# A matmul-tanh-multiply kernel: float32r operands, DMA transposes and 512-column matmuls in place of bf16, TensorE transposes and 384 columns

## The chip, the cores and the metric

The kernel runs on one core of a Trainium2 chip. The metric is device time in microseconds; lower is better. A profiled execution gives a span, from the first to the last instruction, some 2 us below the timed value. Runs of one kernel mostly agree within 0.3%; a run more than 1.5% above the fastest of its kernel is marked slow and left out of comparisons.

Words used below. TensorE multiplies matrices and writes its results into banks of a memory called PSUM. VectorE, ScalarE and GpSimd do the other arithmetic; SyncE, ScalarE and GpSimd also issue DMAs, the transfers between memories, each on a queue of its own. The changed kernel and the experiments pin their instructions to program order, so on an engine or a queue what was written first runs first. float32r is the 4-byte type that the changed kernel gives its matmuls; widening is the copy from bf16 to it. A DMA transpose turns x while it copies it (the crossbar). The DMA share adds up the times of all DMA packets and divides by 16 engines' time; these times can overlap.

## The reference

```python
x: (16, 512, 1024) float32;  w1, w2: (1024, 768) float32
y1 = np.matmul(x, w1); y2 = np.matmul(x, w2)
return (np.tanh(y1) * y2).astype(np.float32)
```

The 16 x 512 rows of x make 64 tiles of 128 rows. Each needs x transposed in eight blocks of 128 x 128, then eight accumulation steps for 768 columns of each weight.

## The kernel before

Weights are loaded as float32 and cast by an engine. x is cast to bf16 by its load, transposed on TensorE, and copied out of PSUM block by block.

```python
nc.sync.dma_start(w1_f, w1r)
nc.sync.dma_start(w2_f, w2r)
# ...
nc.any.tensor_copy(w1_b, w1_f)
nc.any.tensor_copy(w2_b, w2_f)
# ...
for mt in range(MT):
    nc.gpsimd.dma_start(x_b, xf[mt])              # float32 -> bf16
    for ko in range(KO):
        nc.tensor.transpose(pt, x_b[:, ko * P:(ko + 1) * P], ident)
        nc.any.tensor_copy(xT[:, ko, :], pt)
    for nt in range(NT):                          # 2 x 384 columns
        for ko in range(KO):
            nc.tensor.matmul(ps1, xT[:, ko, :], w1_b[:, ko, ns:ns + N_TILE], ...)
            nc.tensor.matmul(ps2, xT[:, ko, :], w2_b[:, ko, ns:ns + N_TILE], ...)
        nc.scalar.activation(t1, ps1, Tanh)
        nc.vector.tensor_tensor(o, t1, ps2, mult)
        nc.sync.dma_start(of[mt, :, ns:ns + N_TILE], o)
```

## Time and profile before

| | before |
|---|---|
| time, us (median of 2) | 414.78 |
| span, us | 413.0 |
| TensorE busy | 92% |
| start to start of 384-column matmuls, ns | 162.5 |
| period of one x tile, us | 6.00 |
| mean clock granted to TensorE, share of full | 0.996 |

The period is the useful line: 64 tiles pass one after the other, and whatever repeats in each tile counts 64 times. The profile lines themselves stand in the prediction.

### The profile page before, as it was taken

The page shows a single profiled execution, that of the slowest core. Times are in us where ns is not written, and L with a number is a line of the kernel's source. Part 1 is how long each engine was busy: PE and PEld are TensorE (multiplying, and loading weights), DVE is VectorE, ACT ScalarE, POOL GpSimd, SP SyncE. Part 2 cuts the span into 40 slices and gives each one's busy share as a digit, 9 for nine tenths or more (in the row PEclk, how much of TensorE's full clock was granted, in tenths as well). Part 3 has the DMA queues.
Part 4 walks back from the last instruction along what each step waited for, and adds up shares of the span by engine and source line. Part 5 has one row for each costly group of instructions (what it writes and reads, how often), then busy time and mean ns, then how long its engine had stood idle before and what let it go on. Part 6 is the DMA issues. An engine that isn't in the chain of part 4 may idle for free.

```text
span 413.0 us, 6572 instructions
## 1 busy us (share of the span) xinstructions
PE 381.2 (92%) x2560; PEld 235.9 (57%) x2560; DVE 107.2 (26%) x316; ACT 128.7 (31%) x455; POOL 36.8 (9%) x70
## 2 busy tenths in 40 slices
PE   1496999999999999999999999999999999999995
PEld 0253666666666666666666666666666666666663
DVE  0301232232223232222323232232223232222322
ACT  1434132332333233323323332332333233323322
POOL 2400001110110011011101101110110011011000
PEclk9998999999999999999999999999999999999999
DMA  8971345444444543444354345434444543444221
GB/s 255 294 264 40 101 123 119 107 108 116 110 109 101 129 109 104 110 108 117 95 128 108 106 106 120 111 102 116 109 110 102 128 106 106 108 110 116 71 77 58
DMA packets 29760, 48.67 MB, mean 118 GB/s; under 512 B 3104, under 2 KB 19488, under 8 KB 29728
## 3 DMA queue, kind: packets, MB, share of 16 engines
q0 software_dynamic: 9216, 16.78, 24.7%
q1 hardware_dynamic: 20512, 31.47, 21.1%
q8 instruction: 20, 0.33, 0.3%
q14 instruction: 12, 0.10, 0.1%
HBM read 39.85 MB, written 25.17 MB: 157 GB/s over the span
## 4 chain that ended last, share of the span: by engine, by line
PE 86%; DMA 7%; DVE 3%; ACT 1%; issue 1%; SPq 0%
PE ps L79 41%; PE ps L77 38%; PE pt L67 7%; DMA w_f<-in_w_dram 7%; DVE xT L68 3%; ACT w_b L53 1%; DVE o L84 0%; ACT t L82 0%; SPq L48 0%
## 5 line engine op out<-in xcount | busy, mean ns | idle before, releaser
L79 PE MATMUL ps<-w_b,xT 128*128 128x384 bf16 x1024 | 326.7, 328 | 4.2 <-ACT w_b L53 4.2
L77 PE MATMUL ps<-w_b,xT 128*128 128x384 bf16 x1024 | 327.0, 328 | 1.6 <-DVE w_b L52 1.6
L82 ACT ACTIVATE t<-ps 128x384 f32<-128x384 f32 x128 | 62.7, 490 | 266.8 <-PE ps L77 263.3
L77 PEld LDWEIGHTS <-xT 128*128 128x128 bf16 x1024 | 100.6, 98 | 77.4 <-issue 19.7
L79 PEld LDWEIGHTS <-xT 128*128 128x128 bf16 x1024 | 100.5, 98 | 67.9 <-issue 6.0
L84 DVE TENSOR_TENSOR o<-t,ps 128x384 f32<-128x384 f32 x128 | 70.9, 554 | 179.7 <-ACT t L82 158.5
L67 PE MATMUL pt<-ident,x_b 128*128 128x128 bf16 x512 | 64.0, 223 | 21.5 <-DMA x_b<-in_x_dram 12.5
L68 ACT COPY xT<-pt 128x128 bf16<-128x128 bf16 x325 | 65.6, 271 | 11.7 <-PE pt L67 11.1
L63 POOL DMA_DIRECT2D x_b<-in_x_dram x64 | 36.2, 566 | 342.9 <-PE pt L67 342.5
L68 DVE COPY xT<-pt 128x128 bf16<-128x128 bf16 x187 | 36.0, 221 | 117.5 <-PE pt L67 114.7
L67 PEld LDWEIGHTS <-x_b 128*128 128x128 bf16 x512 | 39.7, 99 | 26.9 <-DMA x_b<-in_x_dram 13.9
L53 ACT CAST w_b<-w_f 128x6144 bf16<-128x6144 f32 x1 | 5.3, 5312 | 1.0 <-DMA w_f<-in_w_dram 1.0
L52 DVE CAST w_b<-w_f 128x6144 bf16<-128x6144 f32 x1 | 3.4, 3361 | 5.1 <-DMA w_f<-in_w_dram 5.1
L68 ACT ACT_TABLE_LOAD x1 | 1.3, 1283 | 0.7 <-PEq L100 0.7
masks.py:199 POOL TENSOR_SCALAR_AFFINE_SELECT ident<-ident 128x128 bf16<-128x128 bf16 x1 | 0.3, 304 | 0.1
masks.py:197 POOL MEMSET ident<- 128x128 bf16 x1 | 0.2, 204 | 0.3 <-POOLq L100 0.3
L100 POOL MEMSET const-float32-0.0<- 128x1 f32 x1 | 0.1, 98 | 0.2 <-issue 0.2
L100 POOL MEMSET const-bfloat16-1.0<- 128x1 bf16 x1 | 0.1, 102 | 0.0
L100 POOL MEMSET const-uint8-127<- 128x1 uint8 x1 | 0.1, 102 | 0.0
L100 POOL MEMSET const-float32-1.0<- 128x1 f32 x1 | 0.1, 98 | 0.0
## 6 DMA issues: line engine op xcount, KB each, us to landing
out_dram<-o SPq DMA_DIRECT2D x128, 192.0 KB, 1.9
x_b<-in_x_dram POOLq DMA_DIRECT2D x64, 256.0 KB, 3.7
w_f<-in_w_dram SPq DMA_DIRECT2D x2, 3072.0 KB, 22.0
```

The source lines that it names most:

```text
L52: nc.any.tensor_copy(w1_b, w1_f)
L53: nc.any.tensor_copy(w2_b, w2_f)
L63: nc.gpsimd.dma_start(x_b, xf[mt])
L67: nc.tensor.transpose(pt, x_b[:, ko * P:(ko + 1) * P], ident)
L68: nc.any.tensor_copy(xT[:, ko, :], pt)
L77: nc.tensor.matmul(ps1, xT[:, ko, :], w1_b[:, ko, ns:ns + N_TILE], start=st, stop=sp)
L79: nc.tensor.matmul(ps2, xT[:, ko, :], w2_b[:, ko, ns:ns + N_TILE], start=st, stop=sp)
L82: nc.scalar.activation(t1, ps1, mybir.ActivationFunctionType.Tanh)
L84: nc.vector.tensor_tensor(o, t1, ps2, mybir.AluOpType.mult)
L100: nc = _bacc.Bacc("TRN2", target_bir_lowering=False, num_devices=1)
```

## The change

The intent is to leave TensorE only real matmuls: no transposes, wider matmuls, no separate weight cast, and a start that works on four tiles while weights arrive. The diff, cut to its core (the removed lines are those shown above):

```diff
+    w_b = [wpool.tile([P, NC, 2, HALF], f32r, name=f"w_b{k}") for k in range(KO)]
+    pin = tc.keep_in_program_order
+    def load_x(mt):                       # tiles x_b and xT are made here; left out
+        pin(nc.gpsimd.dma_start(x_b, xf[mt]))
+        pin(nc.sync.dma_start_transpose(xT, x_b))
+        xR = xrpool.tile([P, KO, P], f32r, tag="xR", name="xR")
+        pin(nc.vector.tensor_copy(xR, xT))
+        xts[mt] = xR
+    def finish(mt, c, ps, o):
+        pin(nc.scalar.activation(t1, ps[:, :HALF], ACT.Tanh))
+        pin(nc.vector.tensor_tensor(o[:, c * HALF:(c + 1) * HALF], t1, ps[:, HALF:], ALU.mult))
+    def store(mt, o):
+        pin(nc.sync.dma_start(of[mt], o))
... start: four tiles and the weights interleaved, matmuls in order of k, then load_x(4), (5), (6) ...
+    for mt in range(HEAD, MT):            # HEAD = 4
+        if mt + AHEAD < MT:               # AHEAD = 3
+            load_x(mt + AHEAD)
+        o = new_o()
+        for c in range(NC):               # 3 chunks: 256 columns of w1 beside 256 of w2
+            ps = bank()
+            for k in range(KO):
+                mm(ps, mt, k, c)
+            finish(mt, c, ps, o)
+        store(mt, o)
```

## The prediction

> **What bounds the kernel now.** I read the busy line and the chain of the page first.
>
> ```profile
> PE 381.2 (92%) x2560; PEld 235.9 (57%) x2560; DVE 107.2 (26%) x316; ACT 128.7 (31%) x455; POOL 36.8 (9%) x70
> ...
> PE 86%; DMA 7%; DVE 3%; ACT 1%; issue 1%; SPq 0%
> PE ps L79 41%; PE ps L77 38%; PE pt L67 7%; DMA w_f<-in_w_dram 7%; DVE xT L68 3%; ACT w_b L53 1%; DVE o L84 0%; ACT t L82 0%; SPq L48 0%
> ```
>
> TensorE is the bound: 79% of the chain is the two matmul lines, 7% the PE transposes, 3% the copies of transposes that PE waits for, and 8% a start spent on the weight load (DMA) and its cast (ACT). No other engine is above 31%. Next, the groups, and the TensorE timeline of one x tile in the steady part.
>
> ```profile
> L79 PE MATMUL ps<-w_b,xT 128*128 128x384 bf16 x1024 | 326.7, 328 | 4.2 <-ACT w_b L53 4.2
> L77 PE MATMUL ps<-w_b,xT 128*128 128x384 bf16 x1024 | 327.0, 328 | 1.6 <-DVE w_b L52 1.6
> L82 ACT ACTIVATE t<-ps 128x384 f32<-128x384 f32 x128 | 62.7, 490 | 266.8 <-PE ps L77 263.3
> L84 DVE TENSOR_TENSOR o<-t,ps 128x384 f32<-128x384 f32 x128 | 70.9, 554 | 179.7 <-ACT t L82 158.5
> L67 PE MATMUL pt<-ident,x_b 128*128 128x128 bf16 x512 | 64.0, 223 | 21.5 <-DMA x_b<-in_x_dram 12.5
> ```
>
> ```profile
> 54.59 0.75 PE L67 MATMUL pt<-ident,x_b 128*128 128x128 bf16 x5
> 55.18 0.32 PE L77 MATMUL ps<-w_b,xT 128*128 128x384 bf16 x1
> 55.35 0.37 PE L67 MATMUL pt<-ident,x_b 128*128 128x128 bf16 x3
> 55.55 0.32 PE L79 MATMUL ps<-w_b,xT 128*128 128x384 bf16 x1
> 55.72 0.32 PE L77 MATMUL ps<-w_b,xT 128*128 128x384 bf16 x1
> ...
> 60.59 0.75 PE L67 MATMUL pt<-ident,x_b 128*128 128x128 bf16 x5
> ```
>
> The 328 ns of a matmul is a latency; what counts is start to start, 0.162 us here. A tile's period is 60.59 - 54.59 = 6.00 us. It holds 32 matmuls, 32 x 0.1625 = 5.20 us, so the eight transposes and their holes cost 0.80 us. The table of windows agrees: 2203 matmuls of both kinds between 64 and 394 us are 55 tiles of 40 in 330 us, at a granted clock of 1.00. Last the start, from the timeline and the DMA part:
>
> ```profile
> 16.90 3.36 DVE L52 CAST w_b<-w_f 128x6144 bf16<-128x6144 f32 x1 [5.11 <-DMA w_f<-in_w_dram]
> 17.62 2.76 POOL L63 DMA_DIRECT2D x_b<-in_x_dram x1 [1.87 <-PE pt L67]
> ...
> 20.31 9.92 PE L77 MATMUL ps<-w_b,xT 128*128 128x384 bf16 x48 [1.64 <-DVE w_b L52]
> ...
> 29.13 5.31 ACT L53 CAST w_b<-w_f 128x6144 bf16<-128x6144 f32 x1 [0.97 <-DMA w_f<-in_w_dram]
> ```
>
> ```profile
> q0 software_dynamic: 9216, 16.78, 24.7%
> q1 hardware_dynamic: 20512, 31.47, 21.1%
> ```
>
> Real matmuls start at 20.31 us, and the second weight is usable only at 34.4. The steady DMA share is about 45%. A detail for later: the issue of an x load, 0.57 us in the mean, took 2.76 us and ended just after a VectorE cast did.
>
> **What the Trainium skill says.** First, "TensorE: Matmul & The Clock Gate", section Back-to-back issue gap: a warm gap is N / 2.4 + 2.5 ns. For N = 384 this is 162.5, and the trace shows 0.162. For N = 512 it is 215.8 ns. Second, the same page under Weight-path perf modes: the fast weight load is on for 128 weights of a type that is not FP32. Its LDWEIGHTS section gives P / 1.2, so 107 ns for 128 columns. The trace has only bf16 loads, 98 ns each, wholly hidden at N = 384; whether a 4-byte load hides it can't say. Third, "FP8 and Floating Point Precision", section TensorE Precision Notes: a reduced-precision form reads 4-byte data and truncates it to FP22, while true FP32 takes four passes. No run here shows the rate of float32r. Fourth, "DMA: Bandwidth & Descriptors", section Latency and other measured facts: a DMA transpose moves 261 GB/s in one kernel, 350 to 400 where contiguous. The trace before has none.
>
> **The change part by part.**
>
> Matmuls. The columns streamed stay the same: 2048 x 384 = 1536 x 512 = 786,432. The compiled program has 1536 weight loads, each just before its matmul, as before in number of two per product, but the float32r load is one run of 128 columns where the bf16 one is four chunks of 32; I read that as the slow load. At 107 ns it fits below a matmul of 216 ns that streams in front of it, so I take it as hidden and float32r as one column a cycle. Then a tile is 24 x 0.2158 = 5.18 us, and all 1536 are 331.5 us. Wider matmuls by themselves save only 512 x 2.5 ns = 1.3 us.
>
> Transposes on PE. All 512 go, with the holes for their copies: 6.00 - 5.18 = 0.82 us a tile, and 60 steady tiles save 49 us. This is the main gain. The 512 copies on ACT and DVE (101.6 us) go too, off the path.
>
> New work on VectorE. One widening of 1024 elements a tile. The weight cast took 3361 ns for 6144 elements, 0.55 ns each, so 0.56 us (estimate), maybe 0.65 with a fixed part. The products are three of 256 columns instead of two of 384, at most 3 x 554 ns. That is 2.3 us of 5.18. ScalarE has at most 3 x 490 = 1.5 us. Eight PSUM banks are filled at 1.73 us each, so eviction has several banks of slack. Beside PE, nothing on the path.
>
> New work on DMA. q0 took 24.7% of 413 us, 102 us over 64 tiles, so an x load costs all engines 1.6 us; q1's 87 us is mostly stores, at most 1.36 us a tile. The transpose writes 0.262 MB, 1.0 us at 261 GB/s. Sum 4.0 of 5.18 us, a share of 77%. It fits with little to spare. x is fetched three tiles, 15 us, ahead, enough for load (3.7 us to landing), transpose (I guess 3 us) and widening in series.
>
> The start. Four x tiles and eight weight slices come interleaved on one queue. An x tile is 1.6 us; a weight slice of two halves is 0.52 MB, about 1.9 us at the 255 to 294 GB/s that the first slices show. The fourth x tile lands after 4 x 1.6 + 3 x 1.9 = 12.1 us plus 2.5 for issue and latency = 14.6; transpose and widening make it 18.3. The last slice lands near 24. The 64 head matmuls go in order of k, so k = 0 ends near 18.3 and seven groups of 8 x 0.216 = 1.73 follow: 30.5, and about 33.5 with a cold clock at first (3 us). The third column block of these tiles, 32 matmuls, 6.9 us, ends at 40.4; its weights (another 2.1 MB) come in by 32 to 34. Tile 4, loaded after them, is ready near 41.2. Before, tile 4 began one period ahead of 54.59, so about 48.6: a gain of 7.4 us.
>
> Sum. 41.2 + 60 x 5.18 = 352.0, plus a tail of 4.6 us, as in the kernel before from its last tanh at 408.4 to 413.0, is a span of 356.6. The timed value was 1.8 us above the span, so 358.4. By differences: 414.8 - 49.2 - 7.4 = 358.2.
>
> **The rivals.**
> (a) float32r streams at half rate, since each element has twice the bytes. Then 1536 x 0.429 = 659 us plus 30 to 40: near 690. For it: nothing in the trace, which has bf16 alone. Against it: the skill's reduced-precision form is one read, and the change chooses 512 columns and pairs the two weights in one moving operand, as one would who knows the rate holds. I give it 8%.
> (b) The slow weight load isn't hidden. Each matmul then costs 216 + 60 to 107 ns: 1536 x 0.276 to 0.323 = 424 to 496, plus 27, so 450 to 525. For it: a transpose of 128 columns, whose stream is a third of the others', costs 0.59 / 5 = 118 ns start to start, so a load isn't free beside a short matmul. Against it: at 384 columns it is free to the nanosecond, and 107 fits in 216. 8%.
> (c) DMA becomes the bound. If the transpose runs at half the 261 GB/s, the sum is 5.0 us a tile, still just under; at a third it is 6.0, and the kernel takes about 41 + 60 x 6.0 + 6 = 407. SyncE issues transposes and stores in one in-order queue, so a slow issue would show there. 9%.
> (d) VectorE's widening holds up the x loads' issue, as the 2.76 us did. At 0.6 us a tile against three tiles of slack it costs nothing.
>
> **Range and chances.** If (a) to (c) all fail, 75%, the time is 349 to 375: below 349 the start would have to take under 18 us of PE time, above 375 would need stalls in the steady part. A mild (c) reaches 395. So 349 to 390. Faster 0.79, within 2% 0.03 (a hard (c)), slower 0.18.
>
> **What would show each step right or wrong.** Right: matmul starts 0.216 us apart in one tile; tile period 5.18 us; about 96% of the steady chain on the one matmul line; no PE idle on xR after tile 4; DMA share 0.7 to 0.8; first dense matmuls near 18 us, tile 4 near 41. Wrong: starts 0.27 to 0.33 apart with weight loads between, rival (b); 0.43 apart, (a); matmuls waiting for xR and, behind it, for the transposes, (c). A late start would be a wait for x or for weight slices in the first 45 us, and moves the result only by its own length.

## The result

The changed kernel took 469.62 us (468.56 to 470.67) against 414.78: slower, ratio 1.133 (95% interval 1.127 to 1.139). Here and below a ratio is the mean time of one kernel's fast runs over that of the other's in the same rounds, so not quite the ratio of the medians quoted. The prediction of 358 us was far off.

The page of the changed kernel: busy time, the chain that ended last by engine and by line, and groups of instructions (busy us, mean ns, idle time before and what ended it).

```profile
PE 374.1 (80%) x1536; PEld 292.6 (63%) x1536; DVE 108.6 (23%) x256; ACT 68.8 (15%) x193; POOL 54.2 (12%) x100
...
DMA 60%; DVE 13%; PE 11%; issue 8%; SPq 5%; POOL 3%; ACT 0%; DVEq 0%; POOLq 0%
DMA xT<-x_b 54%; DVE o L75 12%; PE ps L84 11%; DMA w_b<-in_w_dram 5%; SPq L81 4%; POOL w_b L59 2%; SPq L67 1%; DMA x_b<-in_x_dram 1%; DVE xR L69 1%; POOL x_b L65 0%; ACT t L74 0%; DVEq L69 0%; POOLq L146 0%
...
L84 PE MATMUL ps<-w_b,xR 128*128 128x512 f32 x1536 | 374.1, 402 | 88.6 <-DVE o L75 61.8
...
L69 DVE CAST xR<-xT 128x1024 fp32r<-128x1024 bf16 x64 | 44.4, 694 | 344.4 <-DMA xT<-x_b 344.3
```

The matmuls, 79% of the chain before, are 11% of it now; the DMA transpose is 54%. VectorE sat idle for 344 us until a transpose landed, and TensorE waited for VectorE's product, which frees a PSUM bank. The queue of SyncE has its own waits (us in total, times, longest):

```profile
SPq L81 <- DVE o L75: 295.0, 64, 7.7
```

So the store (L81) waits on its queue for the product, VectorE waits for the transpose, and the transpose (L67) stands on that same queue. The timeline of two turns in the steady part (start us, us taken, engine, line):

```profile
96.84 0.33 SPq L81 DMA_DIRECT2D out_dram<-o  x1
97.26 1.57 SPq L67 DMA_TRANSPOSE xT<-x_b  x1
101.77 0.69 DVE L69 CAST xR<-xT 128x1024 fp32r<-128x1024 bf16 x1 [4.96 <-DMA xT<-x_b]
...
102.38 1.08 DVE L75 TENSOR_TENSOR o<-t,ps 128x256 f32<-128x256 f32 x3
...
103.48 0.33 SPq L81 DMA_DIRECT2D out_dram<-o  x1
...
103.90 1.74 SPq L67 DMA_TRANSPOSE xT<-x_b  x1
```

Read it as a ring. The transpose is issued at 97.26. It lands 4.5 us later. Only then comes the widening, 0.6 us until the products begin, and the three products, whose inputs had long been ready, 1.1 us. Then the store of that tile, and 0.42 us later the next transpose. The turn is 103.90 - 97.26 = 6.64 us. Between 61.55 us (tile 4's first matmul) and the end of matmuls a tile took 6.68 us in the mean, against 6.00 before.

Two smaller things. Inside a tile float32r matmuls start 227 ns apart, not 216. And tile 4 began at 61.55 us, where the kernel before began the matmuls of its tile 4 at 49.40 (the prediction's 48.6 was an estimate).

Where the 54 us of span went: the start, 61.55 - 49.40 = 12.1, and the 60 tiles after it, 401.1 us against 359.1, which is 42; the tail is 0.4 us shorter.

### The profile page after: what moved, and what is told of

Read it like the earlier page. It is cut to its first block, busy times and chain, and to the rows that moved or that the text cites. A ratio compares the mean times of both kernels' runs of the same rounds, so it can differ in the third digit from the quotient of the medians.

```text
span 466.8 us, 4237 instructions
## 1 busy us (share of the span) xinstructions
PE 374.1 (80%) x1536; PEld 292.6 (63%) x1536; DVE 108.6 (23%) x256; ACT 68.8 (15%) x193; POOL 54.2 (12%) x100
## 3 DMA queue, kind: packets, MB, share of 16 engines
q1 hardware_dynamic: 76800, 41.96, 41.2%
## 4 chain that ended last, share of the span: by engine, by line
DMA 60%; DVE 13%; PE 11%; issue 8%; SPq 5%; POOL 3%; ACT 0%; DVEq 0%; POOLq 0%
DMA xT<-x_b 54%; DVE o L75 12%; PE ps L84 11%; DMA w_b<-in_w_dram 5%; SPq L81 4%; POOL w_b L59 2%; SPq L67 1%; DMA x_b<-in_x_dram 1%; DVE xR L69 1%; POOL x_b L65 0%; ACT t L74 0%; DVEq L69 0%; POOLq L146 0%
## 5 line engine op out<-in xcount | busy, mean ns | idle before, releaser
L84 PE MATMUL ps<-w_b,xR 128*128 128x512 f32 x1536 | 374.1, 402 | 88.6 <-DVE o L75 61.8
L84 PEld LDWEIGHTS ps<-w_b,xR 128*128 128x128 f32 x1536 | 292.6, 193 | 169.7 <-DVE o L75 80.1
L74 ACT ACTIVATE t<-ps 128x256 f32<-128x256 f32 x192 | 67.5, 385 | 393.6 <-DVE o L75 316.6
L69 DVE CAST xR<-xT 128x1024 fp32r<-128x1024 bf16 x64 | 44.4, 694 | 344.4 <-DMA xT<-x_b 344.3
L65 POOL DMA_DIRECT2D x_b<-in_x_dram x64 | 34.3, 546 | 346.6 <-DMA xT<-x_b 345.2
L75 DVE TENSOR_TENSOR o<-t,ps 128x256 f32<-128x256 f32 x192 | 69.1, 415 | 10.5 <-ACT t L74 10.5
L59 POOL DMA_DIRECT2D w_b<-in_w_dram x32 | 20.0, 639 | 11.5 <-DMA w_b<-in_w_dram 9.1
```

The source lines that it names most:

```text
L59: pin(nc.gpsimd.dma_start(w_b[k][:, c0:c1, h, :], src[:, k, c0 * HALF:c1 * HALF].rearrange("p (c j) -> p c j", j=HALF)))
L65: pin(nc.gpsimd.dma_start(x_b, xf[mt]))
L69: pin(nc.vector.tensor_copy(xR, xT))
L74: pin(nc.scalar.activation(t1, ps[:, :HALF], ACT.Tanh))
L75: pin(nc.vector.tensor_tensor(o[:, c * HALF:(c + 1) * HALF], t1, ps[:, HALF:], ALU.mult))
L84: pin(nc.tensor.matmul(ps, xts[mt][:, k, :], w_b[k][:, c, :, :].rearrange("p h j -> p (h j)"), start=k == 0, stop=k == KO - 1))
```

## The experiments

The theory: the loss is the order of instructions. On VectorE the widening of tile mt+3 stands ahead of the products of tile mt; on SyncE's queue the transpose of tile mt+4 stands behind the store of tile mt. Together these make a ring with one transpose per turn, whatever the look-ahead. Rivals: DMA transposes or the DMA engines can't do a tile faster; or float32r itself is what costs. All kernels of the experiments were correct, and before was 412.9 to 416.1 us in all their rounds.

| run | what differs from the changed kernel | us, median (n) | ratio to before |
|---|---|---|---|
| changed kernel | | 469.62 (2) | 1.133 |
| e1_widen_late | widening after the products | 386.26 (4) | 0.932 |
| e2_store_act | stores on ScalarE's queue | 466.84 (4, three slow) | |
| e3_bf16_same_copy | bf16, a copy where the widening was | 463.43 (4) | 1.118 |
| e4_bf16_no_copy | bf16, no copy | 368.64 (4) | 0.888 |
| e5_ahead6 | look-ahead 6 instead of 3 | 475.59 (4) | 1.149 |
| e6_f32r_256 | e1 with 256-column matmuls | 405.86 (1) | one look |
| e7_store_act_2xt | e2, two transposed tiles buffered | 400.77 (4) | 0.970 |
| e9_store_act_3xt | e2, three buffered | 393.92 (4, one slow) | 0.948 |
| e9_store_act_5xt | e2, five buffered | 445.50 (4, three slow) | |
| e8_best | e4 with another start | 354.20 (4) | 0.856 |

### e1_widen_late: the same work, another order on VectorE

```diff
 def load_x(mt):                       # tiles 4 and up; the first four as before
     ...
-    pin(nc.vector.tensor_copy(xR, xT))
+    later[mt] = xT
 for mt in range(HEAD, MT):
     ...
     store(mt, o)
+    if mt + AHEAD < MT:
+        widen(mt + AHEAD, later[mt + AHEAD])    # the tensor_copy
```

Tiles 4 to 6 are widened likewise, each after a store of the first four tiles.

> Everything of the changed kernel is kept (float32r, crossbar transposes, their number, place and queue), only the widening of tile mt+3 stands behind the three products of tile mt in VectorE's order instead of ahead of them. Loop theory (the transpose of a tile is issued behind a store that waits for products that wait behind a widening that waits for the transpose before, so one turn of 4.7 + 0.6 + 1.1 + 0.4 us per tile): the loop is cut, a tile takes 24 x 0.227 = 5.44 us, tile 4 starts near 54 instead of 61.5, and the time is about 54 + 60 x 5.44 + 6 = 387 us. Rival, the crossbar or the DMA engines can't do a tile in less than about 6.7 us: the time stays at 460 to 470. Rival, float32r itself makes the loss: no change either.

Measured: 386.26 us, 83 us below the changed kernel, from moving one instruction per tile. The table of windows for 100 to 360 us (busy us and count per engine, granted clock, DMA share, GB/s) has TensorE busy throughout:

```profile
100.00:360.00 260.00, 260.00 (x1149) 215.36 (x1148) 90.35 (x192) 54.92 (x143) 22.62 (x42) 1.00 0.86 165
```

That is 260 / 1149 = 0.226 us a matmul, so 5.44 us a tile. The transposes now take 5.3 us to land, longer than the 4.7 before, and after the start TensorE waits for nothing. Tile 4 starts at 52.0 us. The ring was the main loss; the transposes and the DMA engines can do a tile in 5.44 us (DMA share 0.86 here, 0.68 in the changed kernel between 100 and 400 us).

The new order doesn't abolish the ring, it makes it longer. A turn of the timeline (start us, us taken, engine, line):

```profile
96.62 0.33 SPq L88 DMA_DIRECT2D out_dram<-o  x1
97.04 1.56 SPq L68 DMA_TRANSPOSE xT<-x_b  x1
...
102.06 0.33 SPq L88 DMA_DIRECT2D out_dram<-o  x1
102.35 0.69 DVE L76 CAST xR<-xT 128x1024 fp32r<-128x1024 bf16 x1 [0.32 <-DMA xT<-x_b]
102.48 1.29 SPq L68 DMA_TRANSPOSE xT<-x_b  x1
```

The transpose issued at 97.04 lands when a whole further tile has been multiplied and stored, and VectorE waits 0.32 us for it. By the program's order such a transpose, issued after the products of tile mt, must land before those of tile mt+2; in the changed kernel it was before those of tile mt+1. So a turn may take two tiles, some 10.9 us.

### e3_bf16_same_copy and e4_bf16_no_copy: is it float32r?

```diff
 e3, e4:
-    w_b = [wpool.tile([P, NC, 2, HALF], f32r, ...
+    w_b = [wpool.tile([P, NC, 2, HALF], bf16, ...
 e3:
-    xR = xrpool.tile([P, KO, P], f32r, ...
+    xR = xrpool.tile([P, KO, P], bf16, ...
 e4:
-    pin(nc.vector.tensor_copy(xR, xT)); xts[mt] = xR
+    xts[mt] = xT
```

> Weights cast to bf16 by the loading DMA, and VectorE makes a plain bf16 copy where the widening stood: the loop is whole, float32r is gone. Loop theory: a tile takes the loop's 6.7 us less what the bf16 copy is shorter (0.69 to perhaps 0.4), so about 6.4, and the time is 440 to 455 us though matmuls could be 0.216 us apart. Rival that float32r matmuls are the loss: 5.2 us a tile, about 370 us.

Measured: 463.43 us. With float32r gone and the ring left, almost nothing is gained, so float32r isn't the main loss. The size was off: 440 to 455 was expected. A tile took 6.61 us. The copy is 0.43 us instead of 0.69, but the transposes landed in 4.9 us instead of 4.7, which took most of that back; why they did is open.

> As the run before but without the copy: TensorE reads the transposed bf16 tile, and VectorE waits for no transpose. Loop theory: cut, 24 x 0.216 = 5.18 us a tile, about 50 + 311 + 6 = 367 us. Against the late widening this is float32r's own price, 11 ns x 1536 = 17 us. Rival of a crossbar or DMA limit: above 430.

Measured: 368.64 us, as expected. Against e1 the difference of 17.6 us is mostly float32r's own price in this kernel: 1536 x 11 ns = 17 us. (The widening and the wider weights go too; the 60 tiles after the start account for 15.6 us.) The windows of 100 to 340 us:

```profile
100.00:340.00 240.00, 240.00 (x1114) 108.81 (x1113) 58.56 (x140) 53.52 (x139) 22.24 (x42) 1.00 0.94 174
```

It is 240 / 1114 = 0.215 us a matmul. The DMA share is 0.94. That isn't a distance to a limit: e8_best, with the same steady part, has 0.88 in the same window, and e2_store_act below has 1.26.

### e6_f32r_256: what the 11 ns are

```diff
 e1, after the start:
-            for k in range(KO):
-                mm(ps, mt, k, c)
+            for h in range(2):
+                for k in range(KO):
+                    matmul(ps[:, h * HALF:(h + 1) * HALF], xts[mt][:, k, :], w_b[k][:, c, h, :], ...)
```

> The late widening with 256-column matmuls after the head (twice as many): what the extra 11 ns of a float32r matmul is. A fixed cost per matmul: [...]120 ns start to start. A share of 5 per cent of the streaming: about 115. A weight load that can't be hidden under a short matmul: clearly above 130, up to the 190 ns that its record lasts. The time is then 54 + 60 x 48 x that gap + 6, so 405 us at 120.

Measured: 405.86 us in one look. The windows of 100 to 360 us, and the group of weight loads:

```profile
100.00:360.00 260.00, 260.00 (x2169) 260.00 (x2169) 86.65 (x182) 51.84 (x135) 23.21 (x43) 1.00 0.84 159
...
L139 PEld LDWEIGHTS ps<-w_b,xR 128*128 128x128 f32 x2880 | 345.7, 192 | 0.1
```

It is 260 / 2169 = 0.120 us. No bf16 run has 256 columns; the line through bf16's 162.5 ns at 384 and 215 at 512 puts it at 110 (an estimate). So the extra looks like a fixed 10 to 11 ns per matmul at both widths, not a share of the streaming, and the weight load is otherwise hidden though its record lasts 192 ns (98 with bf16). What the 11 ns are made of no run shows; they can be a part of the weight load.

### e5_ahead6: more look-ahead

```diff
-    AHEAD = 3
+    AHEAD = 6
```

> The changed kernel with x fetched six tiles ahead instead of three, and the buffers for it. Loop theory: look-ahead buys nothing, for each turn of the loop still carries one transpose; only three more tiles lie outside the loop, each 5.44 instead of 6.7 us, so about 465 us, 460 to 468. Rival, a plain latency that more slack would hide: near 385 us.

Measured: 475.59 us, somewhat above the changed kernel. A latency that slack would hide is thus ruled out. The size was a small miss: the widenings of six tiles, not three, now stand on VectorE ahead of the first four tiles' products, so tile 4 began at 77.4 us instead of 61.5; the 60 tiles after it took 8.8 us less than in the changed kernel (392.3 for 401.1), which doesn't make up for that.

### e2_store_act: the other cut, and what came in its place

```diff
-        pin(nc.sync.dma_start(of[mt], o))
+        pin(nc.scalar.dma_start(of[mt], o))
```

> The changed kernel with the output stores issued from ScalarE's queue, so that on SyncE's queue no transpose stands behind a store; VectorE's order as it was. Loop theory: the other link of the same loop is cut, transposes run ahead by their buffers, 5.44 us a tile, 385 to 400 us in all. Rival of a crossbar or DMA limit: 460 to 470, with transposes back to back on the queue. If only the first of the two cuts helped, the loop as stated would be wrong.

Measured: 466.84 us (452.68 to 477.66, only the lowest of four counted as fast). Even that run is far above the 385 to 400 expected: a plain miss. The trace is of a slow run, 473.04 us. From the DMA part of the page, the queue that now holds the transposes alone (packets, MB, share of 16 engines), and the issues (median us to landing):

```profile
q1 hardware_dynamic: 67584, 16.79, 61.6%
...
x_b<-in_x_dram POOLq DMA_DIRECT2D x64, 256.0 KB, 14.6
...
xT<-x_b SPq DMA_TRANSPOSE x64, 19.2
```

With no store ahead of them, several transposes are under way at once and land after 19 us, and the x loads beside them take 14.6 instead of 3.8. The windows of 100 to 400 us have a DMA share above 1, though no more was moved than in the changed kernel (131 GB/s, 130 there):

```profile
100.00:400.00 300.00, 257.50 (x1068) 206.87 (x1067) 73.64 (x171) 43.28 (x129) 22.07 (x41) 0.95 1.26 131
```

VectorE still waits for each of them in order. Either the transposes pile up and hinder each other, or the store's own queue beside them does harm, or the ring was the wrong cause. The next runs tell these apart by letting fewer transposes be under way.

### e7_store_act_2xt, e9_store_act_3xt, e9_store_act_5xt: how many at once

```diff
 e2 with
-    xtpool = ctx.enter_context(tc.tile_pool(name="xtpool", bufs=HEAD + AHEAD))
+    xtpool = ctx.enter_context(tc.tile_pool(name="xtpool", bufs=2))     # or 3, or 5
```

> The run with stores on ScalarE's queue cut the loop and gained nothing, with transposes landing 19 us after issue and DMA busy throughout. Here the same, with two buffers for the transposed bf16 tile instead of seven, so at most two transposes can be under way. If it was transposes piling up in the queue that took the gain, they now land in about 5 us, a tile takes 5.44 and the time is 385 to 400 us. If it was the store's own queue beside the transposes, or if the loop was the wrong cause, the time stays above 440 us.

Measured: 400.77 us. The same two lines with two buffers:

```profile
q1 hardware_dynamic: 67584, 16.79, 28.8%
...
xT<-x_b SPq DMA_TRANSPOSE x64, 5.3
```

The packets of the same bytes took less than half the time in sum (28.8% of 398.5 us is 115 us; 61.6% of 471.3, in the slow run, is 290). A tile takes 5.44 us. So cutting the ring on SyncE's queue does work, if the transposes don't pile up.

> Between the two runs with stores on ScalarE's queue: two buffers of the transposed bf16 tile gave 400.8 us, seven 466.8. Here three. If queued transposes slow each other step by step, the time is a little above 400, up to 420 us, and the 256-byte packets take longer than 28 ns; if there is a threshold above three it is 400 as with two.

Measured: 393.92 us, with one run of 437.88. Three are as good as two; being a little faster is the start, tile 4 at 61.1 us against 67.7.

> The same with five buffers. If the time grows with the number of transposes that may be under way: between that of three buffers and 466.8 us, 430 to 466, with packets between 28 and 69 ns. If only the last buffers hurt: about 400 us.

Measured: 445.50 us (420.45 to 481.68; only the 420.45 counts as fast). By the fast runs, which are one each for five and seven, the times for two, three, five and seven buffers are about 401, 393, 420 and 453. The slow run with three suggests that three isn't always safe; it has no trace. Before stayed between 412.9 and 416.1 us in the same rounds, so the slow runs here may be the pile-up itself rather than a state of the chip; that isn't shown.

Buffers allowed are not transposes under way. Counted in the traces between issue and landing, three were under way for 67% of the time in e2 and 72% with five buffers (both slow runs), for 12% with three buffers, and in e7 one for 75%. That letting them pile up is harmful is shown: with the stores on the same queue, the number of buffers alone makes 401 or 453 us. Whether the transposes hinder each other or meet more x loads (in e2 two or three of these were under way most of the time, in e7 one) isn't told apart, and why their packets take longer is open.

### e8_best: the start

```diff
 e4 with
+    # w_b[k] is [P, 2, N]: each slice loaded as two rows of 768 columns
+    # the first four tiles:
+    pt = pspool.tile([P, KO, P], bf16, tag="ps", name="pt")
+    for k in range(KO):
+        pin(nc.tensor.transpose(pt[:, k, :], xbs[mt][:, k * P:(k + 1) * P], ident))
+    pin(nc.vector.tensor_copy(xT, pt))
```

> bf16 operands with no copy (368.6 us) with another start: the first four tiles are transposed on TensorE, idle then, so that no crossbar packet shares the DMA engines with the weights, and each weight slice comes as one row of 768 columns. If the late start (tile 4 at 52.5 us) was due to transposes held up among the weight packets, tile 4 starts near 34 to 38 and the time is 350 to 355 us. If the start is bound by the bytes of the weights alone, it stays at 365 to 369.

Measured: 354.20 us, ratio to before 0.856 (0.852 to 0.860). It beats both kernels. Tile 4 starts at 37.3 us instead of 52.5. Both parts of the edit came together, so how much is the transposes' and how much the larger weight loads' isn't told apart. The chain by line is now what the change set out for:

```profile
PE ps L87 94%; DMA x_b<-in_x_dram 2%; POOL w_b L63 1%; POOL x_b L67 0%; PE pt L110 0%; DVE o L78 0%; ACT t L77 0%; POOL ident masks.py:199 0%; POOL ident masks.py:197 0%; POOLq masks.py:199 0%; POOLq L157 0%
```

## Why the prediction was wrong

The predicted span of 356.6 us and the measured 466.8 differ by 110.2 us: 20.4 in the start, 90.3 in the 60 tiles, -0.5 in the tail.

**The step that failed** is that x "is fetched three tiles, 15 us, ahead, enough for load, transpose and widening in series", and with it "Beside PE, nothing on the path" for VectorE. It added up durations per engine and never asked in which order VectorE and SyncE's queue take their instructions. The look-ahead was real for the load from HBM only. The transpose was bound to the store of the tile before, that store to products, and these to a widening that waits for the transpose before. 60 x (6.68 - 5.44) = 74 us are this ring; e1 took it off the path by order alone, and e7 by the other link. The prediction's sign that all is well, "no PE idle on xR after tile 4", came true all the same: TensorE waited for xR four times, all before 31 us, and after the start it waited for the products that free its banks (55.5 us in 42 waits).

**Matmuls at one column a cycle** were right in kind: rivals (a), half rate, and (b), an exposed weight load, both fell. The size was off by 11 ns per matmul, 227 for 215.8, which is the other 60 x 24 x 0.011 = 16 us of the 90. The 4-byte weight load, put at 107 ns, has records of 193 ns and stayed hidden but for at most these 11 ns.

**Removing the transposes from TensorE** was worth what was said: e4, with bf16, has 5.18 us a tile, exactly the figure predicted, and took 368.6 us.

**The DMA sum** was too low. The packets of the transposes took 115 us / 64 = 1.8 us a tile of all engines in e7, not 1.0, and the share with TensorE busy throughout was 0.86 to 0.94, not 0.77. Nor is it a fixed cost that can be added up: the same packets took 290 us in e2. Rival (c) as stated, a DMA bound at 6 us a tile, isn't what happened, since e1 and e4 do a tile in 5.44 and 5.18 us with the same transfers. That rival did name SyncE's in-order queue, but as slow issue; an issue took about 1.5 us, and what mattered was what it stood behind.

**The start** was mis-sized most in one term: a transpose guessed at 3 us. The first was issued at 4.76 us and its widening began at 15.54, among the weight packets; matmuls ran densely from 30.42 us, not from near 18.3. Tile 4 then began at 61.55 instead of 41.2 us. e1 took back 9.5 us of this by no longer holding the first products behind the widenings of tiles 4 to 6, and e8's start 15.1 us of what e4 had.

**Rival (d)**, that the widening would hold up the issue of x loads, didn't show: these took 0.55 us each.

## What to carry to other kernels

When an instruction that waits for a DMA is put into an engine's in-order stream, list what stands behind it, and whether any of that must finish before the next such DMA is issued: if so, look-ahead buys nothing and one DMA latency is paid per turn. Put the waiting instruction behind the work that is ready, which gives the ring another turn's time, and check afterwards that freeing a queue doesn't let transfers pile up. Durations per engine, however well summed, don't show such a ring; the order of each engine's instructions before and after does.

## What the Trainium skill lacked or had wrong

- "DMA: Bandwidth & Descriptors", section Latency and other measured facts, gives 261 GB/s for a DMA transpose, 350 to 400 where contiguous. It lacks a figure for one beside other traffic: here 0.262 MB took 4.7 us from issue to landing, and by the time of its packets (1.8 us a tile in e7) it moved about 146 GB/s. By the same measure the x loads of the kernel before moved 16.78 MB in 102 us, 164 GB/s, so the page isn't shown wrong; no run has a transpose alone.
- No page says what it costs to let several transposes of one queue pile up: with two buffers their packets took 28.8% of the engines' time and they landed in 5.3 us, with seven 61.6% and 19.2 us (a slow run).
- "TensorE: Matmul & The Clock Gate" has no rate for float32r: here 227 ns start to start at 512 columns and 120 at 256 (one look), which is its N / 2.4 + 2.5 and 11 ns more, with weight-load records of 192 ns.
- The same page, section Back-to-back issue gap, gives about 131 ns per matmul as the sustained figure at N = 512 in a stream of weight loads and matmuls, and calls 216 an over-count. e4 shows 240 us / 1114 = 215 ns in just such a stream.
